# Forget gates moved to the head of the mixers, and an output projection taken in two halves of its rows

## The chip, the core and the metric

The kernel runs on one core of one Trainium2 chip. The metric is device time of one execution in microseconds (us), lower is better. The work of the core is spread over engines with queues of their own, each of which runs its instructions strictly in the order in which they were issued: TensorE (PE; its weight loads are listed as PEld), VectorE (DVE), ScalarE (ACT), GpSimd (POOL) and SyncE (SP), whose queue here issues DMA transfers.

## What is computed

A decoder trunk of two layers over 512 positions and 1024 channels. A layer is: feed-forward network, mixing sub-layer, feed-forward network, each with its own RMS norm and added to the residual `x`.

```
h = _rmsnorm(x, mix_norm[i])
x = x + _mixing(h, positions, w_in[i], w_out[i], ...)

def _mixing(...):
    fq, fk, fv, ff, dq, dk, dv, hq, hf, hi, hg = split(h @ w_in)
    c  = cumsum(log_sigmoid(ff + fox_b))               # forget gates, 4 heads
    oa = forgetting attention(fq, fk, fv, c)           # logit[t,s] = q_t.k_s/8 + c[t] - c[s]
    ob = dilated attention(rope(dq), rope(dk), dv)
    oc = _hgrn2(hq, hf, hi) normalised, * hgrn_norm * sigmoid(hg)    # gated recurrence, 4 heads
    return concatenate([oa, ob, oc]) @ w_out
```

`oa` and `ob` have 256 columns each, `oc` has 512: together the 1024 rows of `w_out`.

## The kernel before, in words

All activations are kept channel-first: `x[k]` is a tile of 128 channels x 512 positions, k = 0..7. Products are made in a split fp32r form: every operand is a high part and a low part, and `mm3` issues three TensorE products (high x high, high x low, low x high) for each block of 128 rows of a weight. One product of a 128x128 weight block with 512 positions is called a product below.

**Weights.** `load_split` issues one DMA of 512 KB from the SP queue into `raw` (three buffers), has ScalarE make the high part `wh` (two buffers) and VectorE the low part `wl` (two buffers). These two casts are issued with raised priority. A chunk feeds 24 products.

**Order of work.** A scheduler at build time fixes each engine's order from the order of the code and from priorities; on the chip each engine then follows its list and waits where an operand isn't there. The steps of a mixing sub-layer stand in the code as follows: `decay_inputs`, `values`, `decays`, `states` (the recurrence, for two pairs of heads), `dilated`, `forgetting`, `gated`, and the output projection. The steps run under `run` have priority: a chain of small products, VectorE and ScalarE work (scores `sc_ps`, maximum `nm`, exponential, transposes `pt_ps`, products `po`). The projections of later steps (24 products each: `FFG`, `FQ0`, `FK0`, `FQ1`, `FK1`; 96 each for `V` and `HG`) are put between the pieces of that chain and keep TensorE busy. Their sums stand in four accumulators (`acc`), freed by whoever reads them.

**Forget gates** (`forgetting`, L711 to 727). One projection `FFG`, of which four rows matter; VectorE multiplies by the norm's factor `rb` and adds the bias (`fx`); ScalarE takes the absolute value, an exponential and a logarithm (`fe`); VectorE takes a running sum over 512 positions (the scan, L723) and splits it into `ch` and `cl`. Sixteen small DMAs on the SP queue (L741, L742) copy their rows into the operands `qc` and `kc` of forgetting attention. In the lists of instructions this work stands among the pieces of dilated attention.

**Gates and output.** `gated` projects `HG` and then, for each block b of 128 positions, ScalarE takes a sigmoid into `gate` (one buffer), VectorE multiplies it by the norm weight and the four heads of `ho[b]` by it, and `put_out` transposes the four heads on TensorE into a PSUM bank, always the bank `lv`, out of which ScalarE and VectorE write the parts `ohB`, `olA` of the output. The output projection follows: for each of eight column blocks d it takes a chunk of `w_out` and runs 24 products over the eight row blocks, first two of forgetting attention (`ohf`), two of dilated attention (`ohd`), then four of the recurrence (`ohB`). These last need all four blocks b, since a product runs over all 512 positions. Then x[d] is updated and `after(d)` (split and square for the next norm) is called.

Of the kernel before, what the change touches and what calls it, by code (L numbers as in the profile page):

```python
# [81 lines left out]
def lay_out(inputs):  # L82

    def f(name):
        return np.asarray(inputs[name])

    out = {"x": f("x")[0].T.reshape(KB, 128, T)}
    cols = [f(n)[l].reshape(-1, 128) for n in NORMS for l in range(L)]
    cols += [f("hgrn_lower_bounds")[l].reshape(-1, 128) for l in range(L)]
    out["par"] = np.concatenate(cols).T  # L90
    out["positions"] = f("positions")[0].reshape(NB, 128).T
    for n in ("ffn1", "ffn2"):
        for w in ("gate", "up"):
            a = f(f"{n}_w_{w}").reshape(L, KB, 128, FB, 128)
            out[f"{n}_w_{w}"] = a.transpose(0, 3, 2, 1, 4)
        a = f(f"{n}_w_down")[:L - (n == "ffn2")].reshape(-1, FB, 128, KB, 128)
        out[f"{n}_w_down"] = a.transpose(0, 3, 2, 1, 4)
    a = f("ffn2_w_down")[L - 1].reshape(FB // 2, 2, 128, 2, 512)
    out["last_w_down"] = a.transpose(3, 0, 2, 1, 4)
    w = f("w_in")  # L100
    out["w_in"] = np.stack([
        np.concatenate([rows_first(np.concatenate([w[l, k * 128:(k + step) * 128, c:c + m] for c, m in parts], 1))
                        .ravel() for parts, step in IN_LOADS.values() for k in range(0, KB, step)])
        for l in range(L)])
    a = f("w_out").reshape(L, KB, 128, KB, 128)
    out["w_out"] = a.transpose(0, 3, 2, 1, 4)
    out["fox_forget_bias"] = f("fox_forget_bias").T
    out["hgrn_out_norm"] = f("hgrn_out_norm")
    out["final_norm"] = f("final_norm")
    return {k: np.ascontiguousarray(v) for k, v in out.items()}  # L110
# [19 lines left out]
def hybrid_trunk(ctx: ExitStack, tc: tile.TileContext, a, out):  # L130
# [107 lines left out]
    def load_split(src, n, cols):  # L238

        if raws:  # L240
            raw = raws.pop(0)
        else:
            raw = wp.tile([128, n, cols], F32, tag="raw", name="raw", bufs=3)
            nc.sync.dma_start(out=raw, in_=src)
        with tc.high_priority(AHEAD):
            wh = wp.tile([128, n, cols], R32, tag="wh", name="wh")
            S.copy(wh, raw)  # L247
            wl = wp.tile([128, n, cols], R32, tag="wl", name="wl")
            V.tensor_tensor(out=wl, in0=raw, in1=wh.bitcast(F32), op=ALU.subtract)  # L249
        return wh, wl  # L250
# [213 lines left out]
    def mixing(l, after, r, rb):  # L464
# [34 lines left out]
        def slot(tag, shape, name, dt=F32, bufs=1):  # L499
            return mp.tile(list(shape), dt, tag=tag, name=name, bufs=bufs)  # L500
# [207 lines left out]
            return attend("d", operands, dv, masks[:, 1, :])  # L708


        def forgetting():  # L711
            fv = vv[:, :, 256:512]
            ps = proj_d("FFG", "ff_ps")
            fx = slot("qx", (128, T), "fx")[0:4, :]
            V.tensor_tensor(out=fx, in0=ps[0:4, :], in1=rb[0:4, :], op=ALU.mult)
            V.tensor_scalar(out=fx, in0=fx, scalar1=fbias[0:4, l:l + 1], scalar2=None, op0=ALU.add)
            fe = slot("nw", (128, T), "fe")[0:4, :]
            S.activation(fe, fx, AF.Abs)
            S.activation(fe, fe, AF.Exp, scale=-1.0)
            S.activation(fe, fe, AF.Ln, bias=1.0)  # L720
            V.tensor_scalar(out=fx, in0=fx, scalar1=0.0, scalar2=None, op0=ALU.min)

            V.tensor_tensor_scan(out=fx, data0=fx, data1=fe, initial=0.0, op0=ALU.add, op1=ALU.subtract)  # L723
            ch = slot("nw", (128, T), "ch", R32)[0:4, :]
            V.tensor_copy(ch, fx)
            cl = fx.bitcast(R32)
            V.tensor_tensor(out=cl, in0=fx, in1=ch.bitcast(F32), op=ALU.subtract)


            q2 = [pair(t, f"fq{t}", R32) for t in ("A2", "A6")]  # L730
            k2 = [pair(t, f"fk{t}", R32) for t in ("V0", "V1")]
            qc = [pair(t, f"fqc{t}", R32) for t in ("am", "F0")]
            kc = [pair(t, f"fkc{t}", R32) for t in ("F1",)]
            kc.append(slot("ob", (128, 3, T), "fkcob", R32)[:, 0:2, :])
            for i in range(2):
                G.memset(qc[i][64:68].bitcast(F32), -1.0)
                G.memset(kc[i][64:68].bitcast(F32), 1.0)
                for n in range(2):
                    h = 2 * i + n
                    for part, c in enumerate((ch, cl)):  # L740
                        nc.sync.dma_start(out=qc[i][66 + part:67 + part, n, :].bitcast(F32), in_=c[h:h + 1, :].bitcast(F32))  # L741
                        nc.sync.dma_start(out=kc[i][64 + part:65 + part, n, :].bitcast(F32), in_=c[h:h + 1, :].bitcast(F32))  # L742
                ps = proj_d(f"FQ{i}", "fq_ps")
                u = mp.tile([128, 768], F32, tag="qk", name="fu", bufs=2)[:, 0:T]
                V.scalar_tensor_tensor(out=u, in0=ps, scalar=0.125, in1=rb, op0=ALU.mult, op1=ALU.mult)
                for n in range(2):
                    own, other = slice(64 * n, 64 * n + 64), slice(64 - 64 * n, 128 - 64 * n)
                    S.copy(q2[i][own, n, :], u[own])
                    S.copy(qc[i][0:64, n, :], u[own])
                    V.tensor_tensor(out=q2[i][other, n, :], in0=u[own], in1=q2[i][own, n, :].bitcast(F32),  # L750
                                    op=ALU.subtract)
                ps = proj_d(f"FK{i}", "fk_ps")
                u = mp.tile([128, 768], F32, tag="qk", name="fu", bufs=2)[:, 0:T]
                V.tensor_tensor(out=u, in0=ps, in1=rb, op=ALU.mult)
                for n in range(2):
                    own, other = slice(64 * n, 64 * n + 64), slice(64 - 64 * n, 128 - 64 * n)
                    S.copy(k2[i][own, n, :], u[own])
                    S.copy(k2[i][other, n, :], u[own])
                    V.tensor_tensor(out=kc[i][0:64, n, :], in0=u[own], in1=k2[i][own, n, :].bitcast(F32),
                                    op=ALU.subtract)  # L760
            def operands(h):
                i, n = divmod(h, 2)
                return [(q2[i][:, n, :], k2[i][:, n, :]), (qc[i][0:68, n, :], kc[i][0:68, n, :])]

            return attend("f", operands, fv, masks[:, 0, :])
# [37 lines left out]
            V.tensor_scalar(out=ss, in0=ss, scalar1=1.0 / 128, scalar2=EPS, op0=ALU.mult, op1=ALU.add)  # L803
            hrs[p] = rsqrt(ss.rearrange("p b h -> p (b h)"), [128, 8], f"hr{p}")

        def gated():
            nw = slot("nw", (128, 512), "nw")
            nc.sync.dma_start(out=nw, in_=a["hgrn_out_norm"][l].partition_broadcast(128))
            oth["h"] = [pair(t, f"oh{t}", R32) for t in ("B0", "B1")]
            otl["h"] = [pair(t, f"ol{t}", R32) for t in ("A1", "A4")]  # L810
            pss = proj_t("HG", "hg_ps")
            for b in range(NB):
                gate = slot("gate", (128, 512), "gate")
                S.activation(gate, pss[b], AF.Sigmoid, scale=r[:, b:b + 1])
                V.tensor_tensor(out=gate, in0=gate, in1=nw, op=ALU.mult)
                for h in range(4):
                    V.scalar_tensor_tensor(out=ho[b][:, h, :], in0=ho[b][:, h, :],
                                           scalar=hrs[h // 2][:, b * 2 + h % 2:b * 2 + h % 2 + 1],
                                           in1=gate[:, h * 128:(h + 1) * 128],
                                           op0=ALU.mult, op1=ALU.mult)  # L820
                put_out("h", b, ho[b].rearrange("p h v -> p (h v)"), 4, "lv")


        d0 = decays(0, *decay_inputs(0))
        hv = values()
        run(d0)
# [1 line left out]
        run(decays(1, *decay_inputs(1)))  # L828
        run(states(1, hv))
        run(dilated())  # L830
        f = forgetting()
        oth["f"] = [pair("A0", "ohf", R32)]
        otl["f"] = [pair("A3", "olf", R32)]
        run(f)
        gated()


        rows = [(kind, i) for kind, n in (("f", 2), ("d", 2), ("h", 4)) for i in range(n)]
        for d in range(KB):
            wh, wl = load_split(a["w_out"][l, d], KB, 128)  # L840
            ps = acc("o_ps")
            for k, (kind, i) in enumerate(rows):
                mm3(ps, wh[:, k, :], wl[:, k, :], oth[kind][i // 2][:, i % 2, :],
                    otl[kind][i // 2][:, i % 2, :], k == 0, k == KB - 1)
            V.tensor_tensor(out=x[d], in0=ps, in1=x[d], op=ALU.add)
            after(d)


    offsets = in_offsets()
# [34 lines left out]
```

## Time and profile before

| | |
|---|---|
| time, median of 3 runs | 2086.95 us (2086.71 to 2086.98) |
| profiled execution: its time, its span | 2091.99 us, 2090.2 us |
| TensorE busy, share of the span | 2057.8 us, 98% |
| VectorE, ScalarE busy | 1011.1 us (48%), 727.6 us (35%) |
| mean granted TensorE clock over the span | 0.995 |
| share of TensorE in the chain that ended last | 94% |

The profile is one execution, and its durations are read from a trace of single instructions. A TensorE product that waits shows as idle time ahead of it, with the instruction that released it. A granted clock of 1.00 is full speed (2.4 GHz), 0.50 is the lower level (1.2 GHz), and a value between them is a stretch that had both. The layers are alike: the mixers of the first run from about 372 to 684 us of the span, those of the second from about 1406 to 1715 us.

### The profile page before, as it was taken

Reading aid. Unit: us, or ns where it says so; the run is one execution under the profiler, and the core shown is the slowest. Engines: PE = TensorE matmul, PEld = TensorE weight load, DVE = VectorE, ACT = ScalarE, POOL = GpSimd, SP = SyncE. Lnnn points to the kernel's source line nnn. Section 1 sums busy time; section 2 is a strip of 40 time slices with the busy share of each in tenths; the row PEclk is TensorE's granted clock in tenths of the full one; section 3 lists DMA queues with packets and bytes.
Section 4 is the critical chain, followed back from the end, with each engine's and each line's share of the span. In section 5 each row is a group of like instructions: output and inputs, shape, how many; then the busy total and the mean of one; then the engine's idle time right before and its main releaser. Section 6 shows DMA issues by size and latency. Waiting matters only on the chain.

```text
span 2090.2 us, 23934 instructions
## 1 busy us (share of the span) xinstructions
PE 2057.8 (98%) x9660; PEld 1695.2 (81%) x9660; DVE 1011.1 (48%) x1645; ACT 727.6 (35%) x1104; POOL 13.0 (1%) x18
## 2 busy tenths in 40 slices
PE   8999999999999999999999999999999999999998
PEld 6888888888787888888888888888887778888886
DVE  7544433556555544443354444335565554444333
ACT  5332222333654323322232322232346543322222
POOL 0000000000000000000000000000000000000000
PEclk9999999999999999999999999999999999999999
DMA  4223233211112232333322223332111122232232
GB/s 167 94 99 101 89 101 94 88 63 41 68 50 81 91 101 92 100 96 93 104 91 95 97 101 95 92 106 72 61 51 64 54 81 97 95 101 93 99 101 81
DMA packets 54312, 184.93 MB, mean 88 GB/s; under 512 B 7337, under 2 KB 7465, under 8 KB 54201
## 3 DMA queue, kind: packets, MB, share of 16 engines
q1 hardware_dynamic: 53592, 182.28, 26.9%
q8 instruction: 76, 1.25, 0.2%
q10 hardware_dynamic: 576, 1.05, 0.1%
q14 instruction: 36, 0.29, 0.0%
q0 software_dynamic: 32, 0.07, 0.0%
HBM read 181.21 MB, written 2.10 MB: 88 GB/s over the span
## 4 chain that ended last, share of the span: by engine, by line
PE 94%; DVE 3%; ACT 2%; issue 0%; DMA 0%; SPq 0%; ACTq 0%; DVEq 0%
PE gu_ps L254 15%; PE gu_ps L255 15%; PE gu_ps L256 15%; PE d_ps L254 6%; PE d_ps L256 6%; PE d_ps L255 6%; PE d_ps L429 5%; PE lv_ps L571 2%; PE po L644 2%; PE o_ps L254 1%; PE o_ps L255 1%; PE o_ps L256 1%; PE sc_ps L625 1%; PE pt_ps L637 1%; PE ho_ps L795 1%; PE hf_ps L255 1%
## 5 line engine op out<-in xcount | busy, mean ns | idle before, releaser
L247 ACT CAST wh<-raw 128x1024 fp32r<-128x1024 f32 (+1 forms) x344 | 356.6, 1037 | 1100.0 <-issue 435.9
L254 PE MATMUL gu_ps<-xh,wh 128*128 128x512 f32 x1408 | 549.1, 390 | 7.6 <-ACT wh L247 7.6
L249 DVE TENSOR_TENSOR wl<-raw,wh 128x1024 fp32r<-128x1024 f32 (+1 forms) x344 | 414.2, 1205 | 292.8 <-ACT wh L247 291.1
L256 PE MATMUL gu_ps<-xh,wl 128*128 128x512 f32 x1408 | 550.4, 391 | 0.0
L255 PE MATMUL gu_ps<-xl,wh 128*128 128x512 f32 x1408 | 548.9, 390 | 0.0
L254 PEld LDWEIGHTS gu_ps<-xh,wh 128*128 128x128 f32 x1408 | 265.1, 188 | 63.7 <-ACT wh L247 7.6
L256 PEld LDWEIGHTS gu_ps<-xh,wl 128*128 128x128 f32 x1408 | 264.8, 188 | 56.6 <-issue 1.0
L255 PEld LDWEIGHTS gu_ps<-xl,wh 128*128 128x128 f32 x1408 | 264.8, 188 | 54.9 <-DVE xl L190 0.2
L254 PE MATMUL d_ps<-hh,wh 128*128 128x512 f32 x528 | 205.4, 389 | 0.0
L255 PE MATMUL d_ps<-hl,wh 128*128 128x512 f32 x528 | 205.4, 389 | 0.0
L256 PE MATMUL d_ps<-hh,wl 128*128 128x512 f32 x528 | 205.4, 389 | 0.0
L384 DVE TENSOR_TENSOR u<-gu_ps,rb 128x512 f32<-128x512 f32 x88 | 60.8, 691 | 271.4 <-PE gu_ps L256 271.4
L381 DVE TENSOR_TENSOR g<-gu_ps,rb 128x512 f32<-128x512 f32 x88 | 60.8, 691 | 185.4 <-PE gu_ps L256 179.4
L255 PEld LDWEIGHTS d_ps<-hl,wh 128*128 128x128 f32 x528 | 99.1, 188 | 20.6
L256 PEld LDWEIGHTS d_ps<-hh,wl 128*128 128x128 f32 x528 | 99.1, 188 | 20.6
L254 PEld LDWEIGHTS d_ps<-hh,wh 128*128 128x128 f32 x528 | 99.1, 188 | 20.5
L387 ACT CAST hh<-u 128x512 fp32r<-128x512 f32 x88 | 54.9, 624 | 58.9 <-DVE u L385 58.9
L429 PE MATMUL d_ps<-wl,hh 128*128 128x512 f32 x176 | 69.1, 392 | 0.3 <-DVE wl L249 0.3
L429 PE MATMUL d_ps<-wh,hl 128*128 128x512 f32 x176 | 68.8, 391 | 0.0
L429 PE MATMUL d_ps<-wh,hh 128*128 128x512 f32 x176 | 68.4, 392 | 0.0
L385 DVE TENSOR_TENSOR u<-u,g 128x512 f32<-128x512 f32 x88 | 60.9, 692 | 8.4
L571 PEld LDWEIGHTS lv_ps<-hQ,hk 128*128 128x128 f32 x448 | 55.8, 191 | 8.4 <-issue 6.2
(277 smaller groups left out, 2407.5 us busy)
## 6 DMA issues: line engine op xcount, KB each, us to landing
raw<-in_ffn_w_gate SPq DMA_DIRECT2D x88, 512.0 KB, 3.4
raw<-in_ffn_w_up SPq DMA_DIRECT2D x88, 512.0 KB, 3.4
raw<-in_w_in SPq DMA_DIRECT2D x58, 512.0 KB, 3.4
raw<-in_ffn_w_down SPq DMA_DIRECT2D x48, 448.0 KB, 3.3
raw<-in_ffn_w_down SPq DMA_DIRECT2D x24, 512.0 KB, 3.5
raw<-in_last_w_down SPq DMA_DIRECT2D x22, 512.0 KB, 3.4
raw<-in_w_out SPq DMA_DIRECT2D x16, 512.0 KB, 3.4
x<-in_x SPq DMA_DIRECT2D x8, 256.0 KB, 5.8
```

The lines of the kernel that those rows point to most:

```text
L247: S.copy(wh, raw)
L249: V.tensor_tensor(out=wl, in0=raw, in1=wh.bitcast(F32), op=ALU.subtract)
L254: PE.matmul(ps, lh, rh, start=first, stop=False)
L255: PE.matmul(ps, lh, rl, start=False, stop=False)
L256: PE.matmul(ps, ll, rh, start=False, stop=last)
L381: V.tensor_tensor(out=g, in0=part[0], in1=rb, op=ALU.mult)
L384: V.tensor_tensor(out=u, in0=part[1], in1=rb, op=ALU.mult)
L385: V.tensor_tensor(out=u, in0=u, in1=g, op=ALU.mult)
L387: S.copy(h1, u)
L429: PE.matmul(ps, h[:, s], w, start=first and n == 0, stop=last and n == len(terms) - 1)
L571: PE.matmul(ps[:, e:e + 64], K[:, hh, s], Q[:, hh, s].rearrange("p (n two c) -> p n two c", two=2, c=c)[:, :, 1, :], start=True, stop=True)
L644: PE.matmul(po[:, h * HD:(h + 1) * HD], pt[:, j * 128:(j + 1) * 128], val[:, j, h * HD:(h + 1) * HD], start=j == 0, stop=j == b)
```

## The change

The work on the forget gates becomes a function `forget_gates`, called as the first step of the mixers; its buffers are now the slots `gate` and `nw`. The matrix `w_out` is laid out in chunks of one half of the rows (attention, or recurrence) and two column blocks. `gated` computes all four blocks of the gated result first and is handed a generator, `first_rows`, that issues the attention half for column blocks 0 to 3 around the four transposes, each of which has a PSUM bank of its own. The recurrence half for these blocks, and both halves for blocks 4 to 7, follow.

```diff
-    a = f("w_out").reshape(L, KB, 128, KB, 128)
-    out["w_out"] = a.transpose(0, 3, 2, 1, 4)
+    a = f("w_out").reshape(L, 2, 4, 128, 4, 2, 128)
+    out["w_out"] = a.transpose(0, 1, 4, 3, 5, 2, 6).reshape(L, 2, 4, 128, KB, 128)
...
-        def forgetting():
-            fv = vv[:, :, 256:512]
+        def forget_gates():
             ps = proj_d("FFG", "ff_ps")
-            fx = slot("qx", (128, T), "fx")[0:4, :]
+            fx = slot("gate", (128, T), "fx")[0:4, :]
             V.tensor_tensor(out=fx, in0=ps[0:4, :], in1=rb[0:4, :], op=ALU.mult)
...
             V.tensor_tensor(out=cl, in0=fx, in1=ch.bitcast(F32), op=ALU.subtract)
+            return ch, cl
+
+        def forgetting(ch, cl):
+            fv = vv[:, :, 256:512]
...
-        def gated():
+        def gated(between):
+
             nw = slot("nw", (128, 512), "nw")
...
-                put_out("h", b, ho[b].rearrange("p h v -> p (h v)"), 4, "lv")
-
-
+            for b, bank in enumerate(("lv", "pt", "po", "sc")):
+                next(between)
+                put_out("h", b, ho[b].rearrange("p h v -> p (h v)"), 4, bank)
+            for _ in between:
+                pass
+
+
+        sums = forget_gates()
         d0 = decays(0, *decay_inputs(0))
...
         run(dilated())
-        f = forgetting()
+        f = forgetting(*sums)
         oth["f"] = [pair("A0", "ohf", R32)]
         otl["f"] = [pair("A3", "olf", R32)]
         run(f)
-        gated()
...
-        for d in range(KB):
-            wh, wl = load_split(a["w_out"][l, d], KB, 128)
-            ps = acc("o_ps")
-            for k, (kind, i) in enumerate(rows):
-                mm3(ps, wh[:, k, :], wl[:, k, :], oth[kind][i // 2][:, i % 2, :],
-                    otl[kind][i // 2][:, i % 2, :], k == 0, k == KB - 1)
-            V.tensor_tensor(out=x[d], in0=ps, in1=x[d], op=ALU.add)
-            after(d)
+        pss = {}
+
+        def add_rows(half, pair):
+            wh, wl = load_split(a["w_out"][l, half, pair], KB, 128)
+            for i in range(2):
+                d = 2 * pair + i
+                if not half:
+                    pss[d] = acc("o_ps")
+                for j in range(4):
+                    k = 4 * half + j
+                    kind, n = rows[k]
+                    mm3(pss[d], wh[:, 4 * i + j, :], wl[:, 4 * i + j, :], oth[kind][n // 2][:, n % 2, :],
+                        otl[kind][n // 2][:, n % 2, :], k == 0, k == KB - 1)
+                if half:
+                    V.tensor_tensor(out=x[d], in0=pss[d], in1=x[d], op=ALU.add)
+                    after(d)
+                yield
+
+        def first_rows():
+            for _ in add_rows(0, 0):
+                pass
+            yield
+            yield
+            more = add_rows(0, 1)
+            next(more)
+            yield
+            yield
+            yield from more
+
+        gated(first_rows())
+        for half, pair in ((1, 0), (1, 1), (0, 2), (1, 2), (0, 3), (1, 3)):
+            for _ in add_rows(half, pair):
+                pass
```

On TensorE, behind the last product of `HG`, the list before ran the attention products of blocks d = 0 and 1, with the transposes of block b = 0 ahead of them and those of b = 1 among them; it ended in these rows (`o_ps_4829` and `o_ps_4867` are d = 0 and 1, `ot_ps` is what a transpose writes, `ho1` holds b = 2 and 3):

```order
L255 MATMUL o_ps_4867<-old_2676,wh_4863 128x512
L256 MATMUL o_ps_4867<-ohd_2675,wl_4865 128x512
L515 MATMUL ot_ps_4798<-ident_103,ho1_2683 128x128 x4
L515 MATMUL ot_ps_4814<-ident_103,ho1_2683 128x128 x4
L254 MATMUL o_ps_4829<-ohB0_4631,wh_4825 128x512
L254 MATMUL o_ps_4867<-ohB0_4631,wh_4863 128x512
```

There the last two transposes stood back to back, and directly behind them products that need their results. In the changed list 24 attention products (d = 0 and 1) come straight behind `HG`, then the transposes of b = 0 and 1, then these rows, where `o_ps_4843` and `o_ps_4874` are d = 2 and 3:

```order
L255 MATMUL o_ps_4843<-old_2676,wh_4839 128x512
L256 MATMUL o_ps_4843<-ohd_2675,wl_4841 128x512
L515 MATMUL ot_ps_4856<-ident_103,ho1_2683 128x128 x4
L515 MATMUL ot_ps_4865<-ident_103,ho1_2683 128x128 x4
L254 MATMUL o_ps_4874<-ohf_4347,wh_4839 128x512
L255 MATMUL o_ps_4874<-olf_4348,wh_4839 128x512
```

Twelve attention products (d = 2) now stand ahead of the transposes of b = 2 and 3, and twelve (d = 3) behind them, before the first product that needs `ohB`.

On VectorE, at the third block of dilated attention, the list before had the scan (L723) and its neighbours between the score passes (`ISA neg,nm` and `ISA nm`, L629):

```order
L721 TENSOR_SCALAR fx<-fx 4x512
L629 ISA neg,nm<-sc_ps,masks 128x384
L629 ISA nm 128x1
L649 TENSOR_TENSOR o_3957<-po,den 128x256
L723 SCALAR_TENSOR_TENSOR fx<-fx,fe 4x512
L629 ISA neg,nm<-sc_ps,masks 128x384
L629 ISA nm 128x1
```

The changed list has at the same place the split of the first `FQ` projection (L748, L753) a few rows earlier, and no instruction on `fx`:

```order
L753 TENSOR_TENSOR fqA_4163<-fu,fqA_4163 64x512 x2
L642 COPY pt<-pt_ps 128x256
L647 RECIPROCAL den<-den 128x4
L629 ISA neg,nm<-sc_ps,masks 128x384
L629 ISA nm 128x1
L629 ISA neg,nm<-sc_ps,masks 128x384
L629 ISA nm 128x1
L649 TENSOR_TENSOR o_4000<-po,den 128x256
```

On ScalarE, at the head of the mixers, the copy of `rb` (L235) was followed by a weight cast (L247), one load of a function table (L538) and the sigmoids:

```order
L235 COPY rb<-rb_ps 128x512
L247 CAST wh<-raw 128x1024
L538 ACT_TABLE_LOAD
L538 ACTIVATE hk_2686<-hf_2684 128x1024
L539 ACTIVATE hf_2684<-hf_2684 128x1024
```

Now the three functions of the forget gates and two more table loads stand ahead of them:

```order
L235 COPY rb<-rb_ps 128x512
L717 ACTIVATE fe<-fx 4x512
L247 CAST wh<-raw 128x1024
L718 ACT_TABLE_LOAD
L718 ACTIVATE fe<-fe 4x512
L719 ACT_TABLE_LOAD
L719 ACTIVATE fe<-fe 4x512
L247 CAST wh<-raw 128x1024
L538 ACT_TABLE_LOAD
```

On the SP queue the sixteen row copies go from one block behind the load for `FQ1` to groups of four, four, six and two between earlier weight loads.

## Rows read from the trace of the kernel before

**Rows 1.** Who TensorE waited for, whole execution: us in total, times, longest.

```profile
PE ot_ps L515 <- DVE olA L521: 6.1, 4, 2.4
PE sc_ps L625 <- DVE nm L629: 2.7, 2, 1.3
```

**Rows 2.** TensorE in stretches: from:to us, width, busy (instructions), granted clock, DMA.

```profile
551.00:556.00 5.00, 3.24 (x17) 1.00 0.00 0
556.00:560.00 4.00, 4.00 (x18) 0.57 0.02 2
627.00:641.00 14.00, 11.37 (x54) 1.00 0.22 76
641.00:649.00 8.00, 7.11 (x19) 0.57 0.00 0
1585.00:1590.00 5.00, 3.24 (x17) 1.00 0.00 0
1590.00:1595.00 5.00, 5.00 (x34) 1.00 0.03 3
1659.00:1673.00 14.00, 11.31 (x54) 0.99 0.23 75
1673.00:1680.00 7.00, 6.13 (x17) 0.53 0.01 2
```

**Rows 3.** Timeline of ScalarE, VectorE, TensorE at the forget gates: start, duration, engine, line.

```profile
551.08 1.28 ACT L720 ACT_TABLE_LOAD   x1
552.37 0.63 ACT L720 ACTIVATE fe<-fe 4x512 f32<-4x512 f32 x1
553.02 1.28 ACT L633 ACT_TABLE_LOAD   x1
553.03 1.21 DVE L723 TENSOR_TENSOR_SCAN fx<-fx,fe 4x512 f32<-4x512 f32 x1 [1.41 <-ACT fe L720]
554.76 0.45 PE L625 MATMUL sc_ps<-dkhA,dqB 128*128 128x384 f32 x1 [1.34 <-DVE nm L629]
```

**Rows 4.** Timeline behind the `HG` projection, first layer.

```profile
629.84 1.14 DVE L817 SCALAR_TENSOR_TENSOR ho<-ho,rs_r,gate 128x128 f32<-128x128 f32 x4
630.85 0.60 PE L515 MATMUL ot_ps<-ident,ho 128*128 128x128 f32 x4
631.07 0.69 ACT L814 ACTIVATE gate<-hg_ps,rs_r 128x512 f32<-128x512 f32 x1 [1.99 <-PE hg_ps L496]
631.21 0.47 PE L254 MATMUL o_ps<-ohf,wh 128*128 128x512 f32 x1
631.66 1.05 ACT L247 CAST wh<-raw 128x1024 fp32r<-128x1024 f32 x1
631.79 0.69 DVE L815 TENSOR_TENSOR gate<-gate,nw 128x512 f32<-128x512 f32 x1 [0.81 <-ACT gate L814]
632.79 1.22 DVE L249 TENSOR_TENSOR wl<-raw,wh 128x1024 fp32r<-128x1024 f32 x1
633.92 0.42 DVE L521 TENSOR_TENSOR olA<-ot_ps,ohB 128x256 fp32r<-128x256 f32 x1
641.42 0.91 PE L515 MATMUL ot_ps<-ident,ho 128*128 128x128 f32 x4 [2.41 <-DVE olA L521]
642.79 1.22 PE L254 MATMUL o_ps<-ohB,wh 128*128 128x512 f32 x2 [0.46 <-ACT ohB L520]
```

**Rows 5.** Timeline of TensorE: first and last of 33 products without attention between.

```profile
583.51 0.48 PE L254 MATMUL fk_ps<-xh,wh 128*128 128x512 f32 x1
590.89 0.39 PE L496 MATMUL hg_ps<-wh,xl 128*128 128x512 f32 x1
```

**Rows 6.** Timeline at the head of the mixers, ScalarE and TensorE.

```profile
382.78 0.59 ACT L235 COPY rb<-rb_ps 128x512 f32<-128x512 f32 x1 [3.16 <-PE rb_ps L233]
384.87 0.39 PE L254 MATMUL hq_ps<-xh,wh 128*128 128x512 f32 x1
```

**Rows 7.** Timeline of the SP queue: first and last of the sixteen row copies.

```profile
556.13 0.62 SPq L741 DMA_DIRECT2D fqcam<-ch  x1
566.76 0.59 SPq L742 DMA_DIRECT2D fkcob<-fx  x1
```

## The prediction, made before the changed kernel ran

> **What bounds the kernel.** The table comes first: TensorE is busy for 98% of the span and carries 94% of the chain that ended last, so only what TensorE loses counts, and the other engines count where they make it wait. The list of waits is read next: two of its entries lie in the mixers and repeat per layer, transposes that wait for the gated result (6.1 us in all) and scores of dilated attention that wait for a maximum (2.7 us) [rows 1]. The view by stretches then shows what each place costs, and that a wait costs more than its length. At the forget gates of the first layer 5.00 - 3.24 = 1.76 us are idle, and for the 4 us after that the granted clock is 0.57, a mix of the two levels 1.2 and 2.4 GHz, so TensorE loses (1 - 0.57) x 4 = 1.72 us more; in the second layer the same 1.76 us are idle and the clock stays at 1.00 [rows 2]. Behind `HG` the first layer has 2.63 + 0.89 us idle, then a clock of 0.57 over 7.11 busy us, a loss of 3.06; the second has 2.69 + 0.87 idle and 0.47 x 6.13 = 2.88 [rows 2].
>
> The timelines tell why. At the forget gates ScalarE loads a table (1.28 us), takes the logarithm (0.63) and loads the table for exponentials back (1.28). VectorE stands 1.41 us before its scan, which waits for the logarithm, and the score pass that TensorE needs stands behind the scan; TensorE waits 1.34 us [rows 3]. Behind `HG`, blocks b pass one after another through one `gate` buffer, ScalarE 0.69, VectorE 0.69 and 1.14 us each. TensorE has only the 24 attention products of column blocks 0 and 1 to run meanwhile, waits 2.41 us for the last block, and again 0.46 us for its split [rows 4].
>
> **The change, part by part.** Products are counted at one step: 33 in a row start between 583.51 and 590.89, (590.89 - 583.51) / 32 = 0.231 us [rows 5]. No product, transpose, cast or DMA is added or removed; eight loads of 512 KB per layer remain eight. The most that the two places can give back is the idle time, 2 x 1.76 + 3.52 + 3.56 = 10.6 us, and the lost clock, 1.72 + 3.06 + 2.88 = 7.7 us: 18.3 us. What is left of it after the change has to be found for each part.
>
> *Forget gates, old place.* Scan and table loads leave dilated attention. In their place VectorE and ScalarE do the split of `FQ`, one position earlier than before, in short casts without a table load. That the pieces meet exactly isn't to be expected: I leave 0.3 us idle per layer, between 0 (before, the blocks ahead of and behind this one cost TensorE nothing while the same kinds of casts ran) and 1.76 (all of it). Saved: 2 x 1.46 + 1.72 = 4.6 us.
>
> *Forget gates, new place.* 24 products of `FFG` come ahead of `HF`, so everything behind them on TensorE shifts by 24 x 0.231 = 5.5 us, and the cover of later steps loses as much. That cover has slack: 33 products ran in a row with no piece of either attention between them [rows 5]; 24 of them can go ahead and 9 remain. On ScalarE the new work starts when `rb` is there, at 382.78 + 0.59 = 383.4 [rows 6]. With two VectorE passes of at most 0.69 (the 128x512 pass of [rows 4]; these have 4 partitions), the absolute value (taken as 0.63), a weight cast 1.05, and twice a load of 1.28 and a function of 0.63, the logarithm ends by 390.3, and the next cast by 391.4. VectorE then has the scan 1.21, two short passes of at most 0.69, one 0.69 on `HF` and the low part of the weights 1.22: 394.8. Who waits for these? The products of `HQ1`: `HQ0` began at 384.87 [rows 6], with `FFG` in front `HF1` begins there, and `HQ1` two chunks later, at 384.87 + 11.1 = 396.0. So 1.2 us of slack; I take 0, between 0 and the 1.3 us worked out next.
>
> A rule of the Trainium skill speaks against this place. ScalarE: Activation LUTs, What ACT_TABLE_LOAD costs and the table sets behind it: group the functions by set, because each switch costs the load of about 1.28 us and a drain of about 1.38 us more. This trace agrees on the load, 1.28, but the logarithm starts at 552.37, 1.29 us behind the start of its load at 551.08, with no drain between [rows 3]. With the page's drain in two more switches the low part would come 2.76 us later, at 397.6, and cost TensorE about 1.3 us in each layer: by the page the sum would be 2.6 us smaller, by the row nothing.
>
> *DMAs.* The sixteen row copies held the SP queue from 556.13 to 566.76 + 0.59 = 567.35, 11.2 us in one block ahead of weight loads [rows 7]. Now they go in groups of at most six, 6 x 0.7 = 4.2 us, some of them behind a GpSimd fill that follows the recurrence. What is queued behind them are weight loads that the three raw buffers hold two chunks (11 us) ahead: cost 0. If a group held the queue for longer than that, `FK0` would be late and TensorE with it.
>
> *Gates and first half.* With times of the first layer as if unshifted: block b = 0 is gated at 629.84 + 1.14 = 630.98, and the sigmoid of b = 1 follows at 631.07 [rows 4]. VectorE's list then is: multiply (631.79 to 632.48), one head 0.29, low part of a chunk 1.22, three heads 0.86, so b = 1 is done at 634.9; sigmoid 0.69, multiply 0.69, heads 1.14 and some 0.2 of gaps, b = 2 at 637.6; low part of the next chunk 1.22, multiply 0.69, one `olA` 0.42, heads 1.14: b = 3 at 641.1. TensorE ends `HG` at 630.85, runs 24 products to 636.4, eight transposes (four took 631.21 - 630.85 = 0.36 [rows 4]) to 637.1, 12 products to 639.9, the transposes of b = 2 to 640.2, and waits there for b = 3 until 641.1: **0.9 us idle**, where 2.63 + 0.89 were. Then four transposes and the 12 products of d = 3, to 641.1 + 0.4 + 2.8 = 644.3. Meanwhile VectorE has seven more splits, 7 x 0.42 = 2.9 us, done at 644.1; so the recurrence half finds its operands. Saved: 3.52 + 3.56 - 2 x 0.9 = 5.3 us idle, and the clock losses of 3.06 + 2.88 = 5.9 us, if 0.9 us doesn't pull the clock down. The rows have 1.76 us idle once with a fall and once without, and falls each time behind 3.5 [rows 2]; 0.9 is below all of them, so I take no fall.
>
> *End of the projection.* Column blocks 6 and 7 are now finished 12 products apart, 2.8 us, no longer 24. VectorE has three passes of 0.69 for each and a low part of 1.22 beside them, and the sum of squares for the next norm may come one pass late. I take 0.2 us per layer, between 0 and 0.69.
>
> **Sum.** 4.6 + 5.3 + 5.9 - 2 x 0.2 = 15.4 us. On the profiled execution 2091.99 - 15.4 = 2076.6; it stands 5.04 us above the median, and the same difference on the median gives 2086.95 - 15.4 = **2071.5 us**. With the ends of the small terms (each per layer: gap behind `HG` 0.4 to 1.5, old place 0 to 0.9, end 0 to 0.69) this case spans 2071.5 - 2.0 = 2069.5 to 2071.5 + 3.4 = 2074.9.
>
> **The rivals.**
> - *The clock falls all the same.* The 0.9 us sits at one spot, after three sets of short transposes. If it pulls the clock down, each layer loses between the 1.72 and the 3.06 us of [rows 2]: 2075 to 2077.6. For it: the fall at the forget gates of the first layer followed 1.76 us made of several pieces. Against it: the same idle time without a fall in the second.
> - *Dilated attention still waits.* ScalarE gets three casts in a row ahead of a copy that TensorE waits for; if they cost what the table loads did, 4.6 us are not saved: 2076.1.
> - *The chain of gates stays the end.* VectorE has the low part of one chunk more ahead of b = 3 than before. If this grows and the wait stays at 3.5 us with its clock, the forget gates alone save: 2086.95 - 4.6 + 0.4 = 2082.8, the border of what can be told. Against it: the list above has 24 more products ahead of the same chain.
> - *Cover is missing, slower.* If the attentions need the 24 products that went to the head, TensorE stands 5.5 us in each layer, with a fall as behind `HG` (about 3 us for 3.5 idle): 2071.5 + 2 x 8.5 = 2088.5. It turns slower from 7.7 us per layer. Against it: the 33 products of [rows 5].
>
> **How the numbers follow.** First case 0.62, clock 0.20, dilated 0.10, gates 0.05, cover 0.03. The range 2068 to 2078 holds the first three. A measurement of this kernel can tell about 0.2%, 4.2 us, from no change: faster (below 2082.8) 0.93, same 0.05, slower (above 2091.1) 0.02.
>
> **What the profile will show.** Right: no wait of scores for a maximum at the third block of dilated attention, all its stretch at a clock of 1.00; behind `HG` one wait of about 0.9 us before the last transposes, none before the first product on `ohB`, clock 1.00; three table loads in a row with no TensorE wait at the head. Wrong: a wait of `HQ1` for weights, a clock of 0.5 anywhere in the mixers, or idle time between the attentions.

## The result and the profile after

| | before | after |
|---|---|---|
| median, runs | 2086.98 us, 5 runs (2086.71 to 2091.72) | 2070.79 us, 5 runs (2069.78 to 2071.05) |
| profiled execution: time, span | 2091.99, 2090.2 us | 2069.78, 2068.0 us |
| mean granted clock | 0.995 | 0.999 |

The ratio is 0.9913 (95% interval 0.9902 to 0.9925): 18 us faster, between 15.7 and 20.5 (the two medians alone differ by 16.2). The forecast was 2071.5, in a range of 2068 to 2078. The two profiles differ by 22.2 us of span; the experiments show why that is more than the runs give.

TensorE's waits in the changed kernel, whole execution (who is waited for: us in total, times, longest):

```profile
PE gu_ps L254 <- ACT wh L247: 6.5, 1, 6.5
PE lv_ps L571 <- DVE hk L582: 2.4, 8, 0.3
PE v_ps L494 <- ACT wh L247: 1.3, 2, 0.7
PE v_ps L494 <- ACT qk L669: 0.8, 4, 0.2
PE d_ps L429 <- DVE wl L249: 0.3, 1, 0.3
```

Both waits of [rows 1], `ot_ps` and `sc_ps`, are gone, and none stands in their place: all five entries stood in the list of before too. The longest is the wait for the first weights at the start. TensorE in stretches (from:to, width, busy, granted clock, DMA share, GB/s): the forget gates' old place and the place behind `HG`, both layers:

```profile
541.00:556.00 15.00, 15.00 (x89) 1.00 0.22 71
...
632.00:640.00 8.00, 8.00 (x41) 1.00 0.19 66
640.00:645.00 5.00, 5.00 (x23) 1.00 0.31 105
...
1665.00:1680.00 15.00, 15.00 (x68) 1.00 0.27 88
275.00:325.00 50.00, 50.00 (x222) 1.00 0.33 97
```

Where [rows 2] had 3.24 busy of 5 and clocks of 0.53 and 0.57, TensorE is busy all the time at 1.00. (The last row is a stretch of a feed-forward stage, for the experiments.) The timeline behind `HG` in the first layer, TensorE and VectorE:

```profile
625.48 0.39 PE L496 MATMUL hg_ps<-wh,xl 128*128 128x512 f32 x1
631.15 1.04 PE L515 MATMUL ot_ps<-ident,ho 128*128 128x128 f32 x8
632.24 1.22 DVE L249 TENSOR_TENSOR wl<-raw,wh 128x1024 fp32r<-128x1024 f32 x1
633.39 0.68 DVE L819 TENSOR_TENSOR gate<-gate,nw 128x512 f32<-128x512 f32 x1
634.32 1.13 DVE L821 SCALAR_TENSOR_TENSOR ho<-ho,rs_r,gate 128x128 f32<-128x128 f32 x4
634.78 1.05 PE L515 MATMUL ot_ps<-ident,ho 128*128 128x128 f32 x8
635.59 0.48 PE L254 MATMUL o_ps<-ohf,wh 128*128 128x512 f32 x1
638.43 0.39 PE L254 MATMUL o_ps<-ohB,wh 128*128 128x512 f32 x1
```

The last eight transposes take 635.59 - 634.78 = 0.81 us of TensorE, though block 3's heads are on VectorE until 634.32 + 1.13 = 635.45; the first product on `ohB` follows without a wait. And the head of the mixers, ScalarE, VectorE, TensorE:

```profile
381.54 0.59 ACT L235 COPY rb<-rb_ps 128x512 f32<-128x512 f32 x1 [3.16 <-PE rb_ps L233]
388.21 0.63 ACT L719 ACTIVATE fe<-fe 4x512 f32<-4x512 f32 x1
388.88 1.21 DVE L722 TENSOR_TENSOR_SCAN fx<-fx,fe 4x512 f32<-4x512 f32 x1 [2.66 <-ACT fe L719]
391.78 1.20 DVE L249 TENSOR_TENSOR wl<-raw,wh 128x1024 fp32r<-128x1024 f32 x1
394.99 0.39 PE L256 MATMUL hq_ps<-xh,wl 128*128 128x512 f32 x1
```

The scan waits for the logarithm as before, but nobody on TensorE waits behind it: the low part of `HQ1`'s weights is there at 391.78 + 1.20 = 392.98, 2.0 us ahead of the first product that reads it, at 394.99.

**A measure for what follows.** A mixer stage is taken from the first product on `ss_ps` ahead of it (the row sums of the norm) to the first of the next norm. In the first layer of before, with four more rows of the place behind `HG` (the last product ahead of the waits, the transposes of block 2, and VectorE's last split of block 2 and last two heads of block 3):

```profile
375.76 1.02 PE L219 MATMUL ss_ps<-ones,ss 128*128 128x1 f32 x8
...
637.21 0.40 PE L256 MATMUL o_ps<-ohd,wl 128*128 128x512 f32 x1
638.26 0.76 PE L515 MATMUL ot_ps<-ident,ho 128*128 128x128 f32 x4 [0.65 <-DVE olA L521]
640.85 0.42 DVE L521 TENSOR_TENSOR olA<-ot_ps,ohB 128x256 fp32r<-128x256 f32 x1
641.20 0.61 DVE L817 SCALAR_TENSOR_TENSOR ho<-ho,rs_r,gate 128x128 f32<-128x128 f32 x2
...
687.44 1.05 PE L219 MATMUL ss_ps<-ones,ss 128*128 128x1 f32 x8
```

and of after:

```profile
374.51 1.02 PE L219 MATMUL ss_ps<-ones,ss 128*128 128x1 f32 x8
674.81 1.02 PE L219 MATMUL ss_ps<-ones,ss 128*128 128x1 f32 x8
```

So 311.68 and 300.30 us. In the second layer it is 309.42 and 300.03. The feed-forward stages are equal within 0.1 us (353.8, 361.0, 361.0), and the rest of the span's difference, 1.3 us, is the start.

### The profile page after: what moved, and what is told of

The parts are those of the page before. It is cut to its first block, busy times and chain, and to the rows that moved or that the text cites. A ratio compares the mean times of both kernels' runs of the same rounds, so it can differ in the third digit from the quotient of the medians.

```text
span 2068.0 us, 23940 instructions
## 1 busy us (share of the span) xinstructions
PE 2047.5 (99%) x9660; PEld 1689.0 (82%) x9660; DVE 1010.7 (49%) x1645; ACT 728.9 (35%) x1104; POOL 12.8 (1%) x18
## 4 chain that ended last, share of the span: by engine, by line
PE 96%; DVE 2%; ACT 1%; issue 0%; DMA 0%; SPq 0%; DVEq 0%; ACTq 0%
PE gu_ps L254 15%; PE gu_ps L255 15%; PE gu_ps L256 15%; PE d_ps L255 6%; PE d_ps L256 6%; PE d_ps L254 6%; PE d_ps L429 5%; PE lv_ps L571 2%; PE po L644 2%; PE o_ps L256 1%; PE o_ps L255 1%; PE o_ps L254 1%; PE sc_ps L625 1%; PE pt_ps L637 1%; PE hg_ps L494 1%; PE hg_ps L495 1%
## 5 line engine op out<-in xcount | busy, mean ns | idle before, releaser
L247 ACT CAST wh<-raw 128x1024 fp32r<-128x1024 f32 (+1 forms) x344 | 356.6, 1037 | 1057.4 <-issue 404.4
L256 PEld LDWEIGHTS d_ps<-hh,wl 128*128 128x128 f32 x528 | 99.1, 188 | 20.5
```

The costliest lines, as they stand in the source:

```text
L256: PE.matmul(ps, ll, rh, start=False, stop=last)
```

## The experiments

Twelve kernels, five rounds each, beside runs of before. Over all 58 runs before lies between 2086.7 and 2092.6 us, median 2089.5; the medians beside the three groups of experiments were 2089.8, 2089.2 and 2089.4.

**ctl_before**: no edit.

> The kernel before, unchanged, for a second profile and more times. The profiled execution of before took 2092.0 us, the median of its runs 2087.0. Theory: the 5 us between them are falls of TensorE's clock that come in one execution and not in another, behind the waits that every execution has. Then the runs lie between 2086 and 2092, the idle time of TensorE is the same as in the first profile (sc_ps 1.3 to 1.8 us per layer, ot_ps and o_ps 3.5 per layer), and what differs is the granted clock in the stretches behind it. Rival: the waits themselves differ from run to run; then the idle time differs by several us between the two profiles.

Measured: 2089.41 us, 11 runs (2086.70 to 2092.08). The profile fell on the fastest, 2086.7, span 2084.8. Its list of waits has both lines of [rows 1] with the same numbers. Its stretches, TensorE:

```profile
550.00:555.00 5.00, 3.25 (x17) 1.00 0.00 0
555.00:559.00 4.00, 4.00 (x28) 1.00 0.02 2
626.00:640.00 14.00, 10.81 (x52) 0.97 0.20 70
640.00:648.00 8.00, 7.65 (x29) 0.84 0.04 8
...
1668.00:1675.00 7.00, 5.37 (x18) 0.76 0.01 2
```

At the forget gates 3.25 of 5 busy, as in [rows 2], and the clock stays at 1.00 where it fell to 0.57 there. Reckoned as in the prediction, busy time times what the clock lacks, it costs 10.81 x 0.03 + 7.65 x 0.16 = 1.5 us behind `HG` and 5.37 x 0.24 = 1.3 in the second layer: 2.8 in all (3.0 when only the time at 0.50 is taken), where the first profile has 7.7. The mixers are 4.3 us shorter (308.41 + 308.37 against 311.68 + 309.42), that difference within 0.6 us, and the start 0.9 us. The theory holds: same waits, other falls of the clock.

**gates_only**: of the diff, only `forget_gates()` at the head.

> Only the forget gates go to the head of the mixers; the output projection is that of before. Theory (two separate stalls, each removed by its own part): the wait of the scores for the maximum in dilated attention goes, the waits behind HG stay at 3.5 us per layer with their clock; 4.6 us faster than before by the rows, up to 5.7 by the stage lengths of the changed kernel: 2081 to 2082.5. Rival (24 products of cover are lost to the attentions or to the recurrence): a wait appears elsewhere in the mixers, gain below 2 us. Rival (the gain belongs to the output projection alone): 2087.

Measured: 2083.65 us, 6 runs (2083.07 to 2084.44), ratio 0.9971 (0.9959 to 0.9982): 6.1 us faster, a little more than the 4.6 to 5.7 expected; the time lies above 2081 to 2082.5 because the runs beside it stand at 2089.8 and not at 2087. Of the two waits of [rows 1] this one is left:

```profile
PE ot_ps L515 <- DVE olA L521: 6.1, 4, 2.4
```

`sc_ps` is gone, `ot_ps` untouched, and no wait came elsewhere.

**halves_only**: of the diff, only `w_out`'s layout, `gated(between)` and `add_rows`; the forget gates in `forgetting()` as before.

> Only the output projection in two halves with its four banks; the forget gates stay in dilated attention. Theory: no wait behind HG in either layer and a clock of 1.00 there, the 1.8 us at the forget gates stay with their clock; 11 to 14 us faster than before: 2073 to 2076. Rival (the parts need each other, since the products of the forget gates ahead of everything change what is ready when): less than 8 us. The gains of the two parts alone should add up to that of both, 16.2 us.

Measured: 2076.77 us, 5 runs (2076.58 to 2077.27), ratio 0.9938 (0.9925 to 0.9950): 13.0 us faster, within the 11 to 14 expected. Of the two waits of [rows 1] this one is left:

```profile
PE sc_ps L625 <- DVE nm L629: 2.7, 2, 1.3
```

The mirror image. This part holds two things, the new order and a bank for each block; they weren't run apart on the changed order. 6.1 + 13.0 = 19.1, and both together gave 18.8 in the next group: the parts don't need each other.

**no_log**, on before: it leaves out the logarithm.

```diff
-            S.activation(fe, fe, AF.Ln, bias=1.0)
+            S.copy(fe, fe)
```

> The kernel before with the logarithm of the forget gates replaced by a copy, so that the decay sums are computed from exp(-|x|) instead of log(1 + exp(-|x|)): a changed part of the computation. Two table loads of 1.28 us and a function of 0.63 become one copy per layer; scan, casts, products and row copies stay where they are. Theory (the stall comes from the two table loads in the middle of attention's chain): TensorE's wait for sc_ps there falls from 1.3 us to below 0.3 in each layer and the clock stays at 1.00, 3 to 5 us faster than before, 2082 to 2084. Rival (VectorE's scan of 1.21 us and the small passes make the stall): the wait stays above 1 us, 2087.

Measured: 2083.88 us, 6 runs (2082.96 to 2084.26), ratio 0.9970 (0.9959 to 0.9982), and no `sc_ps` among the waits. Scan, casts and products stay in their old place and yet the wait is gone: what stalled was the logarithm behind its table load, and the load back (the three together; they weren't taken apart). This takes out 5.9 us, as much as moving it all (6.1).

**ctl_after**: the changed kernel, no edit.

> The changed kernel, unchanged, as the base of the three others. Theory: the executions of before differ by up to 5.4 us because falls of the clock behind the same waits come or don't come (two profiles of before: the same waits, 2.7 us sc_ps and 7.0 us ot_ps and o_ps, but 17.1 and 6.8 us at half clock). Without these waits nothing is left to vary: all runs within 1.5 us, 2069.5 to 2071.2, clock 1.00 in the mixers again. Rival (a chip or a moment sets the falls): runs spread over 3 us or more here too.

Measured: 2070.41 us, 4 runs (2070.09 to 2070.70), ratio 0.9910 (0.9897 to 0.9924), the same five waits (the first 7.1). The spread of 6 us is gone with the waits.

**banks_only**, on before:

```diff
-                put_out("h", b, ..., 4, "lv")
+                put_out("h", b, ..., 4, ("lv", "pt", "po", "sc")[b])
```

> The kernel before with its four transposed results behind HG in the four PSUM banks that the change uses, one each, where all went through one; forget gates, projection and weight loads as before. Theory (24 products of cover and a chain of gates that ends with block 3 decide; the bank does not): the heads of block 3 end at the same time, the 2.4 us wait becomes a wait for the heads, at most 0.5 us per layer gained: 2088 to 2090 against 2089.5. Rival (the split of one block holds the bank for the next block's transposes): the wait halves and the time falls by 4 us or more, as much as a third of the gain of the halves.

Measured: 2089.68 us, 11 runs (2087.06 to 2091.72), ratio 1.0001 (0.9992 to 1.0010). Waits:

```profile
PE ot_ps L515 <- DVE ho L817: 4.9, 8, 1.7
```

The wait is now for the heads (`ho`), no longer for the split: in less of listed time, in eight pieces, and at no gain. The bank alone wasn't the limit. In before it came free at 640.85 + 0.42 = 641.27, and the last heads were done at 641.20 + 0.61 = 641.81: behind the bank stands the chain of gates.

**two_gates**, on before: blocks 1 and 3 get a second gate buffer.

```diff
-                gate = slot("gate", (128, 512), "gate")
+                gate = (slot("qx", (128, 2, 256), "gate1").rearrange("p a c -> p (a c)")
+                        if b % 2 else slot("gate", (128, 512), "gate"))
```

> The kernel before with a second gate buffer for blocks 1 and 3 behind HG; all else as before. Theory (TensorE waits there for a chain of gates that VectorE and ScalarE run through one buffer, and has only 24 products meanwhile): ScalarE's sigmoids of blocks 2 and 3 no longer wait for VectorE, 0.76 and 0.75 us of VectorE's idle time before the multiplies go, so the wait behind HG falls from 3.5 to about 2 us per layer; 3 us faster from idle time alone, up to 6 with the clock: 2084 to 2087 against 2089.8. Rival (the chain isn't the end, but the one PSUM bank or the transposes are): no change, 3.5 us stay.

Measured: 2086.60 us, 11 runs (2083.65 to 2089.09), ratio 0.9987 (0.9978 to 0.9995). Waits:

```profile
PE ot_ps L515 <- DVE olA L521: 4.2, 4, 1.9
```

6.1 to 4.2, 0.95 us per layer where 1.5 was expected, and 2.6 us faster. The timeline of the first layer says what the rest is:

```profile
637.88 0.61 DVE L818 SCALAR_TENSOR_TENSOR ho<-ho,rs_r,gate 128x128 f32<-128x128 f32 x2
640.04 0.42 DVE L521 TENSOR_TENSOR olA<-ot_ps,ohB 128x256 fp32r<-128x256 f32 x1 [0.44 <-ACT ohB L520]
640.61 0.63 PE L515 MATMUL ot_ps<-ident,ho 128*128 128x128 f32 x4 [1.88 <-DVE olA L521]
```

The last heads are done at 638.49, 2.1 us ahead of the transposes that read them. What these wait for is the one PSUM bank, which the split of block 2 frees at 640.46. So two chains end close together behind `HG`: take away the bank's (banks_only) and the gates' remains, shorten the gates' and the bank's remains. Both together on the old order weren't run, so how much of the gain of the halves could be had without the halves is open.

**gate_plus**, on after:

```diff
                 V.tensor_tensor(out=gate, in0=gate, in1=nw, op=ALU.mult)
+                V.tensor_scalar(out=gate, in0=gate, scalar1=1.0, scalar2=None, op0=ALU.mult)
```

> The changed kernel with one more VectorE pass of 0.69 us on each of the four gates (times 1.0). The chain of gates grows by 4 x 0.69 = 2.8 us per layer; the scheduler puts nine of the last twelve products of the first half ahead of the last transposes. In the profile of the changed kernel the last block was ready at about the moment when its transposes came up. Theory (cover only just suffices): TensorE now waits 1.3 to 2.8 us behind HG in each layer, 2073.5 to 2076.5, and with falls of the clock as in before up to 2081. Rival (there is slack left, the chain is far from the path): 2070.8, no wait.

Measured: 2072.06 us, 4 runs (2071.65 to 2072.34), 1.6 us over ctl_after, between the two theories. The pass was cheaper than I had priced it, on the timeline:

```profile
632.03 0.69 DVE L819 TENSOR_TENSOR gate<-gate,nw 128x512 f32<-128x512 f32 x1 [0.76 <-ACT gate L818]
632.76 0.43 DVE L820 TENSOR_SCALAR gate<-gate 128x512 f32<-128x512 f32 x1
```

With one tensor operand this pass took 0.43, with two 0.69. So the chain grew by 4 x 0.43 = 1.7 us; the mixers grew by 0.7 (301.01) and 0.9 (300.90), with the clock at 1.00. It isn't the changed list with a longer chain alone: eight of the twelve products of d = 3 now run ahead of block 3's transposes and two among them, where all twelve ran behind.

**gate_plus3**, on after: three such passes.

> The changed kernel with three more VectorE passes on each of the four gates (times 1.0), 0.43 us each by the trial with one: the chain of gates is 12 x 0.43 = 5.2 us longer per layer, with one it was 1.7 us longer, cost 0.75 us per layer and brought no wait above 0.3 us. Theory (cover only just suffices: the last block is ready when its transposes come up): idle time of about 5.2 - 1.7 = 3.5 us per layer behind HG, 2077 from that alone, and the clock falls there again as in before, 1.7 to 3.4 us per layer: 2080 to 2084. If no fall comes, 2077 to 2078. Rival (the scheduler's reordering or other slack hides the chain): below 2073.

Measured: 2081.10 us, 5 runs (2080.67 to 2082.18), 10.7 us over ctl_after. Waits:

```profile
PE o_ps L254 <- ACT gate L818: 2.1, 4, 0.7
PE ot_ps L515 <- DVE ho L823: 1.7, 2, 0.9
...
PE o_ps L254 <- ACT ohB L520: 1.2, 2, 0.8
```

The mixers are 306.53 and 304.66 us; the first layer has a fall of the clock (1.7 us), the second none. Without it the layers lost 4.5 and 4.6 us for a chain 5.2 longer, where 3.5 were expected; with a fall in one layer and not in two the time still came out in the range of 2080 to 2084. Here all twelve products of d = 3 run ahead of block 3's transposes. And the waits for `gate` show a second way in which the chain holds TensorE: products of d = 2 and 3 need an accumulator, and those of `HG` come free only when the sigmoid has read them. As the order differs, neither run measures the slack of the changed kernel. Its own timeline has next to none at the last head, done at 635.45, 0.14 us ahead of the product behind the transposes: the cover suffices, but barely.

**more_tables**, on after: four more table switches at the head.

```diff
+            for i in range(2):
+                tiny = lines(small, [128, 1], tag="tiny", name="tiny")[0:4, :]
+                S.activation(tiny, fe[:, 0:1], AF.Ln)
+                S.activation(fe[:, 0:1], tiny, AF.Exp)
             S.activation(fe, fe, AF.Ln, bias=1.0)
```

> The changed kernel with two tiny detours of the first token's exp(-|x|) through a logarithm and back between the exponential and the logarithm at the head of the mixers: four table loads and four functions of 4x1 more per layer. By the trace a load costs 1.28 us and the function behind it starts 1.29 us after the load's start; so the logarithm comes 4 x 1.28 = 5.1 us later and four times a short function, 0.2 to 0.6 us each by no row. The changed kernel's low part of HQ1's weights was done 2.0 us ahead of its product. Theory: TensorE waits 3.9 to 5.5 us less what VectorE makes up, some 4 us, for HQ1 in each layer: 2078 to 2082, with falls of the clock up to 2088. By the rule of the Trainium skill, ScalarE: Activation LUTs, What ACT_TABLE_LOAD costs, each switch would drain another 1.38 us: 5.5 us more per layer, 2089 and above. Rival (slack above 6 us): 2070.8.

Measured: 2098.35 us, 5 runs (2096.92 to 2099.58): 28 us over ctl_after, while TensorE's waits for `hq_ps` were 4.7 + 2.4 = 7.1 us. The untouched feed-forward stages were 3.5 us longer each (357.3, 364.5). The time fitted a drain (2089 and above), but these waits, 3.6 us per layer, fitted the theory without one; hence the next two.

**more_tables2**: the same with `tiny` in unused partitions of `fx`'s tile.

> The detour of four table loads and four 4x1 functions per layer at the head once more, with the small results in free partitions of an existing tile, so that no tile is added and none moves in SBUF. In the first trial TensorE waited 1.2 and 2.4 us for HQ1 in each layer, the functions took 0.20 us each, and all other stages, the untouched feed-forward ones too, were 3.5 us longer. Theory (the 3.5 us per feed-forward stage come from the shifted addresses and have nothing to do with the tables): the feed-forward stages are back at 353.8 and 361.0 us, the waits at HQ1 stay at 3.6 us per layer, so 2070.5 + 7 = 2077.5, with falls of the clock up to 2084. Rival (the detour itself slows what follows): about 2098 again.

Measured: 2082.78 us, 5 runs (2081.47 to 2083.44), between the 2077.5 without and the 2084 with falls of the clock; feed-forward stages back at 353.8 and 361.0. ScalarE and TensorE at the head:

```profile
387.25 1.28 ACT L721 ACT_TABLE_LOAD   x1
388.54 0.20 ACT L721 ACTIVATE fx<-fe 4x1 f32<-4x1 f32 x1
388.76 1.28 ACT L722 ACT_TABLE_LOAD   x1
390.06 0.20 ACT L722 ACTIVATE fe<-fx 4x1 f32<-4x1 f32 x1
...
396.22 0.50 PE L254 MATMUL hq_ps<-xh,wh 128*128 128x512 f32 x1 [1.20 <-ACT wh L247]
399.31 0.50 PE L256 MATMUL hq_ps<-xh,wl 128*128 128x512 f32 x1 [2.37 <-DVE wl L249]
```

A switch with a tiny function costs 388.76 - 387.25 = 1.51 us. The Trainium skill (ScalarE: Activation LUTs, What ACT_TABLE_LOAD costs) adds a drain of about 1.38 us to each; between these rows there is none. Four make 6.0 us. The mixers grew by 5.5 and 5.8 us, of which the clock is 1.7 each (0.86 on the average of the 12 us from 396, and of the same place in the second layer). That leaves 4.0 us idle per layer, so 6.0 - 4.0 = 2.0 us of slack at the head, as read above.

**shift**, on after:

```diff
-PAD = 96
+PAD = 128
```

> The changed kernel with its padding tile 128 bytes per partition longer, 128 elements in place of 96, which moves the tiles of the feed-forward and the mixer pools by 128 bytes; no instruction is added, removed or moved. Theory (where a tile lies sets how long a product reads it): the four feed-forward stages 3.5 us longer each, some 14 us in all and one or two more in the mixers, 2084 to 2087. Rival (it was the added tile in the pool of small tiles, or the detour): 2070.5.

Measured: 2085.89 us, 11 runs (2085.45 to 2086.75), 15.5 us over ctl_after, with the same waits. The same stretch of a feed-forward stage as in the last row of stretches of after:

```profile
275.00:325.00 50.00, 50.00 (x216) 1.00 0.33 97
```

216 products in 50 us in place of 222, both without a gap at full clock. The three feed-forward stages between norms are 3.5 us longer each, the stretch behind the last norm 2.5, the mixers 1.3 each. So of the first trial's 28 us, 2098.35 - 2082.78 = 15.6 went when the added tile went, and an address alone makes 15.5; the other 12.4 are the switches with their waits and the clock, and no drain. That the added tile moved the same tiles as the padding is argued from the equal size of the effect, not shown.

## Why the prediction was right, and where it was not

**The two stalls and what feeds them: right.** Each part alone takes away its own wait and leaves the other (gates_only, halves_only). That the logarithm with its two table loads makes the first is shown by no_log. That a chain of gates longer than its cover makes TensorE wait is shown by two_gates, which shortens it, and by gate_plus3, which lengthens it. But the prediction saw only the gates, and two_gates shows the one bank as a second chain that ended almost with them; the change took it away too, by its four banks, which no term of the sum had. The list of waits also had more entries in the mixers than the two that the prediction read: `pt_ps` (0.8), `po` (0.3) and `o_ps` (0.9) belong to the same stalls and went with them; `lv_ps` and `v_ps` stayed.

**The size, in its own steps.** Take the mixers of both layers and subtract the clock's cost, half of the time that TensorE was busy while the clock stood at 0.50 (15.4 us in the first profile of before, 6.0 in ctl_before, 9.8 in gates_only, 3.4 in halves_only). What is saved is counted from the mean of the two profiles of before, 613.6:

| kernel | mixers, both layers | clock | rest | saved |
|---|---|---|---|---|
| before, first profile | 621.1 | 7.7 | 613.4 | |
| ctl_before | 616.8 | 3.0 | 613.8 | |
| gates_only | 614.0 | 4.9 | 609.1 | 4.5 |
| halves_only | 606.5 | 1.7 | 604.8 | 8.8 |
| after | 600.3 | 0 | 600.3 | 13.3 |

So 13.3 us are idle time, 4.5 + 8.8, and the remaining 5.5 of some 18.8 us are mostly the clock: the two profiles of before, with 7.7 and 3.0, lie 2.5 us above and 2.8 below the median of its runs. The prediction had 7.8 idle (10.6, less 2.8 that it left over) and 7.7 of clock.

- *Forget gates, old place*: 4.6 forecast, 6.1 measured (3.8 to 8.6). The 0.3 us left per layer didn't come; the split of `FQ` fits in whole.
- *Forget gates, new place*: cost 0, right. The 1.3 us per layer that the prediction reckoned for a drain would be 2.76 - 1.2 = 1.6 by its own numbers; no drain came. Slack forecast 1.2, found 2.0: from the start of `rb` to the end of the low part 11.4 us (392.98 - 381.54) where 12.0 were reckoned, since short passes priced at 0.69 took 0.40 to 0.68, and the product 13.45 us behind `rb`, not 13.2.
- *DMAs*: 0, right, no wait for weights in the mixers that the kernel before doesn't have.
- *Gates and first half*: **the failed step is the 0.9 us** that TensorE should have waited for block 3. The list has the heads done at 641.1, 10.2 us behind the end of `HG` (630.85); they were done at 635.45, 9.7 behind 625.71 (625.48 + 0.23). About half of that 0.5 us is from adding up listed times: passes on VectorE start up to 0.1 us before the listed end of the one ahead (block 3's gate starts at 633.39, and the low part ahead of it is listed until 632.24 + 1.22 = 633.46). And it let the four transposes start when the fourth head is done, though each reads one head: they run between the heads, and the next product starts 0.14 us after the last. Two small lumps made a wait. Taken away, it is worth 1.8 us of the sum.
- *End of the projection*: 0.2 us forecast, none seen (from 660 to 675 us TensorE is busy 15.00 of 15).
- *What is idle*: the row counts idle time from the modelled end of the instruction before. The four transposes at 638.26 are shown until 639.02, and the next wait of 2.41 ends at 641.42 [rows 4]; start to start that is 3.16, less 0.36 of work 2.8 us. The Trainium skill says of TensorE that the profiler computes the end time and doesn't observe it (Perfetto Trace Analysis, Tensor Engine Instruction); the trace agrees, by 0.39 us at this place. Start to start the three waits behind `HG` are 638.26 - 637.21 - 0.23 = 0.82, 2.80 and, with slower transposes in it, 642.79 - 641.42 - 0.36 = 1.01, together 4.6 us where the rows have 3.52. In all it is 13.3 against 10.6.

**The number was better than its working.** 15.4 us were forecast and some 18.8 gained, but from a base of 2086.95, three runs at the low edge of what 58 runs put at 2089.5. The base was 2.6 us too low, the gain 3.4 too small, and the errors cancelled: that is luck. The rule "2091.99 stands 5.04 above the median" took for an offset of the profile what is mostly the clock of one execution. So 7.7 us of clock were taken off a base whose own executions lose about 3.0, as ctl_before at 2086.7 shows: 4.7 too many, against 13.3 - 7.8 = 5.5 us of idle time too few.

**The rivals.** The clock didn't fall again in the mixers, and there was no gap; gate_plus3 shows that it can with 4.5 us of gaps in pieces, in one layer of two. Attention doesn't wait, the cover isn't missing. The chain of gates is the nearest: lengthened by 1.7 us it costs 0.8 per layer, by 5.2 it costs 4.5, each time with the order changed beside it.

## What to carry to other kernels

Price a stall start to start, and let a wait's clock cost be a range, not one profile's number; before summing on a median of three, see how far the profiled run lies from it. A function of another table in the middle of a latency-bound chain cost its loads there and nothing where ScalarE had slack; products that don't need the late operand are cover, if their weights can be in place apart from the others and their accumulators are free. Where two chains end close together, here a gate buffer and a PSUM bank, an experiment that shortens one shows little: read what the wait that is left is for. When an experiment adds a tile, look at a stage that it shouldn't touch.

## What was not expected of the hardware

- Moving tiles by 128 bytes in SBUF slowed products: 216 in place of 222 over the same 50 us, 3.5 us more in each feed-forward stage between norms, 15.5 us in all. Which operand's address does it, and whether any other move does, wasn't tried.
- One pattern of waits gave different clocks: after the same 1.75 us idle at the forget gates 0.57 in one execution and 1.00 in another; gate_plus3's 4.5 us, in pieces of which the longest is listed with 0.9, brought a fall in one layer and none in the other. What decides it stays open.
